# Seven-product block pairs in all output groups of a hybrid decoder layer

## The chip, the cores and the metric

The kernel runs on one core of a Trainium2 chip. The metric is the device time of one execution in microseconds (us). A fixed part of some 2 us lies around the span that the profiler records.

## The reference, cut to what matters

One decoder layer on 256 positions of width 4096, in float32:

```python
def hybrid_layer(x, norm_w, w_in, ..., w_out):
    h = rms_norm(x, norm_w)
    proj = jnp.einsum('bsd,de->bse', h, w_in)           # 4096 -> 13328 columns
    (rq, rk, rv, rg, mq, ..., lx, lg) = jnp.split(proj, ...)
    y_ret  = retention(rq, rk, rv, ret_gn_w) * silu(rg)
    y_moba = moba_attention(mq, mk, mv) * silu(mg)
    y_ssm  = mamba2_ssd(sz, sxbc, sdt, ...)
    y_lru  = rg_lru(lx, ...) * silu(lg)
    y = jnp.concatenate([y_ret, y_moba, y_ssm, y_lru], axis=-1)
    return x + jnp.einsum('bse,ed->bsd', y, w_out)      # 4096 -> 4096

# and behind the layer
out = rms_norm(x, final_norm_w)
```

The change lies in the last product, `y @ w_out`, and in what follows it.

## The kernel before, in words

Both large products keep float32 accuracy by splitting each operand into a high part of type fp32r and the rest (`xT` or `yhl` for the activations, `whi` and `wlo` for the weights). Each block product is then three matmuls: high by high, low by high, high by low. ScalarE (ACT) casts a raw weight tile to `whi` (L187), VectorE (DVE) subtracts to get `wlo` (L188), and TensorE (PE) runs the three matmuls of 128x128 weights by up to 512 columns.

The weights come as chunks of 256 rows by 512 columns (512 KB): two blocks of 128 rows side by side in a raw tile of 1024 columns. One list, `chunks`, holds them in the order of use. At each chunk the loop calls `split(n + SPL)`, which casts and subtracts the chunk two places ahead, and `load(n + RAW)`, which issues on SP's queue the DMA of the chunk four places ahead. There are `RAW` = 4 raw buffers and `SPL + 1` = 3 pairs `whi`, `wlo`. So a cast waits for the PE to leave the chunk before, and a load waits for the last reader of the raw buffer that it takes.

The output has eight groups of 512 columns (`o` = 0 to 7) with 16 chunks each, and two halves of 128 positions (`e` = 0, 1). In the order of time:

- Groups 0 and 1 run alone: per chunk 2 halves x 2 blocks x 3 = 12 matmuls. Between them `mix_y` forms from five chunks of `y` the sums that the pairs need (`ys`).
- Groups 2, 3 and 4, 5 run as pairs (`pair`), chunk by chunk. In 11 of the 16 chunks both groups take 12 matmuls each. In the five chunks of `FAST` = (2, 4, 7, 9, 12) the 2x2 block product (two blocks of rows by two groups, for two halves) is formed by seven block products in place of eight: 21 matmuls in place of 24 (Strassen's scheme in Winograd's form). For it DVE forms four sums of the raw weights in place (L177 to L180), and the two raw tiles are then cast and subtracted once more, whole, into `thi` and `tlo` (three buffers each). The products by themselves (`p1`, `p5`, `p6`, `p7`) gather in four PSUM banks of their own, the others in the four banks of the result. Behind the last such chunk `early` adds them to the residual tiles `xres`, two steps at each chunk (L843).
- Group 6 runs alone, then group 7 with a lag: its half `e` = 1 runs six chunks behind half 0, in pieces of 256 columns, from split tiles that are held (`hhi`, `hlo`), and six chunks of it are left when half 0 is done.

Each finished result goes through `row`: add to `xres` (DVE), square with a sum (ACT), multiply by the norm's weight into `rs` (DVE). At the end of a half, `store` gathers the sum, GpSimd (POOL) takes the power -1/2 (L803), DVE scales the half's 4096 columns in nine pieces (L806), and ACT and SP issue the DMAs of each piece to HBM.

The order of the instructions on each engine is set when the program is built: a scheduler places them from the program's order and its own costs, and each engine then runs its list in order.

Of the kernel before, what the change touches and what calls it, by code (L numbers as in the profile page):

```python
# [93 lines left out]
def tile_kernel(ctx: ExitStack, tc: tile.TileContext, t: dict):  # L94
# [64 lines left out]
    def split(n):  # L159
        if n >= len(chunks):  # L160
            return
        where, _, kt, nk, w = chunks[n]
# [3 lines left out]
        c = kt // KC
        pool, tag, bufs, size = wp, "w", SPL + 1, WW
        if where == "last" and c % (SPL + 1 + HOLD) > SPL:
            pool, tag, bufs, size = holds[0], "h", HOLD, KC * 512
# [582 lines left out]
    fsm = fp.tile([P, 64], F32, name="fsm")  # L752
# [26 lines left out]
    def mms(ps, e, c, p, c0=0, c1=512):  # L779
        hi, lo = p  # L780
        for k in range(KC):
            kt = c * KC + k
            x, a, b = yhl[kt], k * 512 + c0, k * 512 + c1
            xh, xl = x[:, e * P:(e + 1) * P], x[:, 256 + e * P:256 + (e + 1) * P]
            T.matmul(ps[:, c0:c1], xh, hi[:, a:b], start=kt == 0, stop=False)  # L785
            T.matmul(ps[:, c0:c1], xl, hi[:, a:b], start=False, stop=False)  # L786
            T.matmul(ps[:, c0:c1], xh, lo[:, a:b], start=False, stop=kt == KT - 1)  # L787
# [40 lines left out]
    def three(ps, x, p, at, first, last):  # L828

        hi, lo = p[0][:, at:at + 512], p[1][:, at:at + 512]  # L830
        T.matmul(ps, x[0], hi, start=first, stop=False)
        T.matmul(ps, x[1], hi, start=False, stop=False)
        T.matmul(ps, x[0], lo, start=False, stop=last)

    def pair(o, n, q, r):
# [147 lines left out]
```

## Time and profile before

| | |
|---|---|
| median of 3 runs | 1567.84 us (1567.80 to 1570.99) |
| the profiled execution | 1566.89 us |
| its span | 1565.1 us |
| PE busy | 1550.7 us, 99% |
| DVE busy | 910.9 us, 58% |
| ACT busy | 764.9 us, 49% |
| output product and what follows, within the span | from 1206.8 to 1565.1 us |

Matmuls are pipelined, and their ends are modelled: a matmul of 512 columns is shown with some 390 ns, while in an undisturbed stretch the next one starts 227 ns behind it. So the length of a stretch divided by its count of matmuls says more than the mean of one. The granted clock was at its upper level (1.00) throughout the products.

### The profile page before, as it was taken

What the parts mean: (1) busy time and instruction counts of PE and PEld (TensorE: products, weight loads), DVE (VectorE), ACT (ScalarE), POOL (GpSimd) and SP (SyncE); (2) the same over time, 40 slices, a digit from 0 to 9 for tenths busy, and PEclk for the clock granted to TensorE, in tenths of its full rate; (3) what the DMA queues carried; (4) which work ended last, traced back from release to release, by engine and by line L of the source; (5) the groups of instructions that cost most, each with busy time, mean ns of one, the idle gap of its engine ahead of it and who ended that gap; (6) DMA issues with size and microseconds to landing.
All of it is one profiled execution on the core that took longest, in us unless ns stands there. A gap on an engine that the chain in (4) does not pass through costs nothing.

```text
span 1565.1 us, 19219 instructions
## 1 busy us (share of the span) xinstructions
PE 1550.7 (99%) x7304; PEld 1292.6 (83%) x7304; DVE 910.9 (58%) x1132; ACT 764.9 (49%) x965; POOL 28.2 (2%) x56
## 2 busy tenths in 40 slices
PE   9999999999999999999999999999999999999997
PEld 8988888888888788888888888888888888777886
DVE  6564444475565644454557657444456747887754
ACT  6744444454454434444548845444446444554441
POOL 0000000000000100000000000000000000000000
PEclk9999999999999999999999999999999999999999
DMA  8965555555555655555555455555555666565763
GB/s 308 334 207 188 176 176 185 183 189 188 200 184 188 212 178 188 175 175 177 188 193 177 167 201 182 193 190 189 189 186 191 230 217 209 199 216 194 261 228 143
DMA packets 89133, 311.20 MB, mean 199 GB/s; under 512 B 10304, under 2 KB 11984, under 8 KB 89040
## 3 DMA queue, kind: packets, MB, share of 16 engines
q1 hardware_dynamic: 83808, 296.70, 54.9%
q0 software_dynamic: 3360, 10.51, 2.3%
q10 hardware_dynamic: 1872, 2.76, 0.5%
q8 instruction: 57, 0.93, 0.2%
q14 instruction: 36, 0.29, 0.1%
HBM read 305.71 MB, written 4.22 MB: 198 GB/s over the span
## 4 chain that ended last, share of the span: by engine, by line
PE 94%; DVE 2%; DMA 2%; ACT 1%; issue 1%; POOL 0%; ACTq 0%; POOLq 0%; DVEq 0%
PE pm L704 24%; PE pm L703 24%; PE pm L702 24%; PE pm L786 4%; PE pm L785 4%; PE pm L787 4%; PE pb L786 2%; PE pb L785 2%; PE pb L787 2%; PE pb L279 1%; DMA raw<-in_wo 1%; DVE wlo L188 1%; ACT whi L187 1%; PE pb L704 0%; PE pb L703 0%
## 5 line engine op out<-in xcount | busy, mean ns | idle before, releaser
L188 DVE TENSOR_TENSOR wlo<-raw,whi 128x1024 fp32r<-128x1024 f32 (+3 forms) x538 | 648.1, 1207 | 576.6 <-ACT whi L187 551.8
L187 ACT CAST whi<-raw 128x1024 fp32r<-128x1024 f32 (+3 forms) x538 | 556.1, 1035 | 678.8 <-PE pm L703 496.6
L702 PE MATMUL pm<-whi,xT 128*128 128x512 f32 (+1 forms) x1664 | 645.6, 388 | 1.4 <-ACT whi L187 1.4
L704 PE MATMUL pm<-wlo,xT 128*128 128x512 f32 (+1 forms) x1664 | 641.9, 386 | 0.8 <-DVE wlo L188 0.8
L703 PE MATMUL pm<-whi,xT 128*128 128x512 f32 (+1 forms) x1664 | 641.4, 386 | 0.0
L702 PEld LDWEIGHTS pm<-whi,xT 128*128 128x128 f32 x1664 | 312.7, 188 | 64.1 <-ACT whi L187 1.9
L704 PEld LDWEIGHTS pm<-wlo,xT 128*128 128x128 f32 x1664 | 312.2, 188 | 64.4 <-DVE wlo L188 1.6
L703 PEld LDWEIGHTS pm<-whi,xT 128*128 128x128 f32 x1664 | 312.6, 188 | 61.8
L786 PE MATMUL pm<-whi,xT 128*128 128x512 f32 (+1 forms) x252 | 95.7, 380 | 0.0
L787 PE MATMUL pm<-wlo,xT 128*128 128x512 f32 (+1 forms) x252 | 95.6, 379 | 0.0
L785 PE MATMUL pm<-whi,xT 128*128 128x512 f32 (+1 forms) x252 | 95.6, 379 | 0.0
L785 PE MATMUL pb<-whi,xT 128*128 128x512 f32 x152 | 59.2, 389 | 0.0
L786 PE MATMUL pb<-whi,xT 128*128 128x512 f32 x152 | 59.2, 389 | 0.0
L787 PE MATMUL pb<-wlo,xT 128*128 128x512 f32 x152 | 59.1, 389 | 0.0
L785 PEld LDWEIGHTS pm<-whi,xT 128*128 128x128 f32 x252 | 47.4, 188 | 9.0
L786 PEld LDWEIGHTS pm<-whi,xT 128*128 128x128 f32 x252 | 47.4, 188 | 9.0
L787 PEld LDWEIGHTS pm<-wlo,xT 128*128 128x128 f32 x252 | 47.4, 188 | 8.9
L785 PEld LDWEIGHTS pb<-whi,xT 128*128 128x128 f32 x152 | 28.5, 188 | 6.0
L787 PEld LDWEIGHTS pb<-wlo,xT 128*128 128x128 f32 x152 | 28.5, 188 | 5.9
L786 PEld LDWEIGHTS pb<-whi,xT 128*128 128x128 f32 x152 | 28.5, 188 | 5.9
L271 ACT ACTIVATE y<-pm,rstd 128x512 f32<-128x512 f32 x24 | 16.5, 687 | 14.7 <-PE pm L704 14.7
L188 DVE TENSOR_TENSOR tlo<-raw,thi 128x1024 fp32r<-128x1024 f32 x20 | 23.6, 1219 | 0.0
(272 smaller groups left out, 982.8 us busy)
## 6 DMA issues: line engine op xcount, KB each, us to landing
raw<-in_w SPq DMA_DIRECT2D x384, 512.0 KB, 3.5
raw<-in_wo SPq DMA_DIRECT2D x128, 512.0 KB, 4.4
raw<-in_w SPq DMA_DIRECT2D x31, 520.0 KB, 4.4
b<-in_x SPq DMA_DIRECT2D x8, 512.0 KB, 5.1
xres<-in_x POOLq DMA_DIRECT2D x16, 256.0 KB, 5.5
b<-in_xt SPq DMA_DIRECT2D x15, 257.0 KB, 4.5
fw<-in_fnw POOLq DMA_DIRECT2D x8, 256.0 KB, 5.7
out<-rs ACTq DMA_DIRECT2D x8, 256.0 KB, 2.9
```

The costliest lines, as they stand in the source:

```text
L187: A.copy(hi[:, a:b], raw[:, a:b])
L188: V.tensor_tensor(lo[:, a:b], raw[:, a:b], hi[:, a:b].bitcast(F32), ALU.subtract)
L271: A.activation(tk[k], ps[k], func, scale=rstd[:, k:k + 1])
L279: T.transpose(ps[:, e * S + k * P:e * S + (k + 1) * P], tk[k][:, (2 * u + e) * P:(2 * u + e + 1) * P], ident)
L702: T.matmul(ps[:, :w], xh, hi[:, o:o + w], start=first, stop=False)
L703: T.matmul(ps[:, :w], xl, hi[:, o:o + w], start=False, stop=False)
L704: T.matmul(ps[:, :w], xh, lo[:, o:o + w], start=False, stop=last)
L785: T.matmul(ps[:, c0:c1], xh, hi[:, a:b], start=kt == 0, stop=False)
L786: T.matmul(ps[:, c0:c1], xl, hi[:, a:b], start=False, stop=False)
L787: T.matmul(ps[:, c0:c1], xh, lo[:, a:b], start=False, stop=kt == KT - 1)
```

## The change

All eight output groups run as pairs (0 1, 2 3, 4 5, 6 7). Pair 0 has three chunks with seven products (7, 9, 12), the others five, 18 in all in place of 10. Chunks of both groups of a pair alternate in the list. `mix_y` runs at the chunks 1 to 5 of pair 0. The four banks for the result and the four for the separate products change places from pair to pair.

In a seven-product chunk the two raw sum tiles are cast and subtracted in halves of 512 columns, each as soon as its sum stands, into four buffers. There are five raw buffers in place of four, and room is made by a smaller area for the descriptors of POOL's DMAs (`dynamic_dma_scratch_size`).

Group 7 no longer runs with a lag. In the last pair the half `e` = 1 of the chunks 13 to 15 is left until half 0 is done (`held`): group 6 in whole rows of 512 columns, group 7 in two pieces of 256 in the banks `spare`. The rows of half 0 are finished and stored between.

```diff
-SPL, RAW, HOLD, WARM = 2, 4, 6, 28
+SPL, RAW, WARM = 2, 5, 28
-PAIRS, FAST = (2, 4), (2, 4, 7, 9, 12)
+FAST = {0: (7, 9, 12), 2: (2, 4, 7, 9, 12), 4: (2, 4, 7, 9, 12), 6: (2, 4, 7, 9, 12)}
+LATE = 13
...
+    for o in FAST:
+        for c in range(NCH):
+            for i in range(2):
+                where = "fast" + "ab"[i] if c in FAST[o] else "hold" if o == NO - 2 and LATE <= c + i / 2 < LATE + 1.5 else "out"
+                chunks.append((where, t["wo"][o + i, c], KC * c, KC, 512))
...
-            a = raws.pop("a")
-            V.tensor_tensor(a[:, 0:512], raw[:, 0:512], a[:, 0:512], ALU.subtract)
-            V.tensor_tensor(raw[:, 0:512], raw[:, 512:1024], raw[:, 0:512], ALU.subtract)
-            V.tensor_tensor(raw[:, 512:1024], raw[:, 512:1024], a[:, 0:512], ALU.subtract)
-            V.tensor_tensor(a[:, 512:1024], a[:, 512:1024], raw[:, 512:1024], ALU.subtract)
-            parts[n, "t"] = [high_low(r, ((0, 1024),), mixed[0], "t", 3, 1024) for r in (a, raw)]
...
+            ra, rb = raws.pop("a"), raw
+            (ha, la), (hb, lb) = (pair_of(mixed[0], "t", 4, 1024) for _ in range(2))
+            c1, c2 = slice(0, 512), slice(512, 1024)
+            V.tensor_tensor(ra[:, c1], rb[:, c1], ra[:, c1], ALU.subtract)
+            V.tensor_tensor(rb[:, c1], rb[:, c2], rb[:, c1], ALU.subtract)
+            high_low(ha, la, ra, 0, 512)
+            V.tensor_tensor(rb[:, c2], rb[:, c2], ra[:, c1], ALU.subtract)
+            high_low(hb, lb, rb, 0, 512)
+            V.tensor_tensor(ra[:, c2], ra[:, c2], rb[:, c2], ALU.subtract)
+            high_low(hb, lb, rb, 512, 1024)
+            high_low(ha, la, ra, 512, 1024)
+            parts[n, "t"] = (ha, la), (hb, lb)
...
-                if c not in FAST:
-                    for e in range(2):
-                        mms(q[2 * e + i], e, c, p)
-                    continue
...
+                else:
+                    mms(q[i], 0, c, p, c == 0, c == NCH - 1)
+                    if end and c >= LATE:
+                        held[c, i] = p
+                    else:
+                        mms(q[2 + i], 1, c, p, c == 0, c == (LATE - 2 if end and i else NCH - 1))
...
+        row(o, 0, q[0], x11, fw1, o)
+        row(o + 1, 0, q[1], x12, fw2, o + 1, 0, 256)
+        done = store(0)
+        row(o + 1, 0, q[1], x12, fw2, NO, 256, 512)
+        done()
+        for c in range(LATE, NCH):
+            mms(q[2], 1, c, held[c, 0], False, c == NCH - 1)
+        row(o, 1, q[2], x21, fw1, o)
+        for j, a in enumerate((0, 256)):
+            for c in range(LATE, NCH):
+                mms(spare[j], 1, c, held[c, 1], c == LATE, c == NCH - 1, a, a + 256)
+            row(o + 1, 1, spare[j], x22, fw2, NO if j else o + 1, a, a + 256)
+            if j == 0:
+                done = store(1)
+        done()
...
-    nc = bacc.Bacc("TRN2", target_bir_lowering=False, num_devices=1)
+    nc = bacc.Bacc("TRN2", target_bir_lowering=False, num_devices=1, dynamic_dma_scratch_size=4096)
```

DVE's list in the kernel before, from the splits ahead of a pair's first seven-product chunk on. The names are those of the sections above; L188 is the subtraction of a split, L177 to L180 are the four sums:

```order
L188 TENSOR_TENSOR wlo<-raw,whi 128x1024 x3
L177 TENSOR_TENSOR raw<-raw 128x512
L178 TENSOR_TENSOR raw<-raw 128x512
L188 TENSOR_TENSOR wlo<-raw,whi 128x512
L179 TENSOR_TENSOR raw<-raw 128x512
L180 TENSOR_TENSOR raw<-raw 128x512
L188 TENSOR_TENSOR wlo<-raw,whi 128x1024
L188 TENSOR_TENSOR tlo<-raw,thi 128x1024 x2
L188 TENSOR_TENSOR wlo<-raw,whi 128x1024 x2
```

The same place in the changed kernel, where L174 is the subtraction of a split and L186, L187, L189 and L191 are the sums:

```order
L174 TENSOR_TENSOR wlo<-raw,whi 128x1024 x3
L186 TENSOR_TENSOR raw<-raw 128x512
L187 TENSOR_TENSOR raw<-raw 128x512
L174 TENSOR_TENSOR wlo<-raw,whi 128x512
L174 TENSOR_TENSOR tlo<-raw,thi 128x512
L189 TENSOR_TENSOR raw<-raw 128x512
L174 TENSOR_TENSOR tlo<-raw,thi 128x512
L191 TENSOR_TENSOR raw<-raw 128x512
L174 TENSOR_TENSOR wlo<-raw,whi 128x1024
L174 TENSOR_TENSOR tlo<-raw,thi 128x512 x2
L174 TENSOR_TENSOR wlo<-raw,whi 128x1024 x2
```

The two whole subtractions into `tlo` became four halves, and two of them moved ahead of the last sums.

DVE's list in the changed kernel behind the last seven-product chunk of the last pair. `tlo` of 1024 columns are the held splits of the chunks 13 and 14, L843 are the additions of `early`:

```order
L174 TENSOR_TENSOR tlo<-raw,thi 128x1024
L843 TENSOR_TENSOR xres<-xres,ma 128x512
L174 TENSOR_TENSOR tlo<-raw,thi 128x1024
L843 TENSOR_TENSOR ma<-ma,pm 128x512
L174 TENSOR_TENSOR wlo<-raw,whi 128x1024
L843 TENSOR_TENSOR mb<-ma,pm 128x512
L174 TENSOR_TENSOR wlo<-raw,whi 128x1024
L843 TENSOR_TENSOR xres<-xres,ma 128x512
L174 TENSOR_TENSOR wlo<-raw,whi 128x1024
L843 TENSOR_TENSOR xres<-xres,pm 128x512
L843 TENSOR_TENSOR xres<-xres,mb 128x512 x2
L804 TENSOR_TENSOR xres<-xres,pb 128x512
```

In the kernel before, the splits at this place stood alone, with no additions between or behind them.

DVE's list in the kernel before from the first row piece of half 0 in group 7 on (L791 and L793 are the two DVE steps of `row`, L806 the scaling, `rs_9407` half 0 and `rs_9408` half 1):

```order
L791 TENSOR_TENSOR xres<-xres,pm 128x256
L793 TENSOR_TENSOR rs_9407<-xres,fw 128x256
L797 TENSOR_REDUCE fsm<-fsm 128x1
L791 TENSOR_TENSOR xres<-xres,pm 128x256
L798 TENSOR_SCALAR fsm<-fsm 128x1
L793 TENSOR_TENSOR rs_9407<-xres,fw 128x256
L802 TENSOR_TENSOR fsm<-fsm 128x1
L806 TENSOR_SCALAR rs_9407<-rs_9407,fsm 128x256 x2
L806 TENSOR_SCALAR rs_9407<-rs_9407,fsm 128x512 x7
L791 TENSOR_TENSOR xres<-xres,pm 128x256
L793 TENSOR_TENSOR rs_9408<-xres,fw 128x256
```

The same place in the changed kernel (L804, L806, L819 stand for L791, L793, L806; `rs_9409` is half 0, `rs_9410` half 1):

```order
L804 TENSOR_TENSOR xres<-xres,pb 128x256
L806 TENSOR_TENSOR rs_9409<-xres,fw 128x256
L810 TENSOR_REDUCE fsm<-fsm 128x1
L804 TENSOR_TENSOR xres<-xres,pb 128x256
L811 TENSOR_SCALAR fsm<-fsm 128x1
L804 TENSOR_TENSOR xres<-xres,pb 128x512
L806 TENSOR_TENSOR rs_9409<-xres,fw 128x256
L815 TENSOR_TENSOR fsm<-fsm 128x1
L806 TENSOR_TENSOR rs_9410<-xres,fw 128x512
L819 TENSOR_SCALAR rs_9409<-rs_9409,fsm 128x256 x2
L819 TENSOR_SCALAR rs_9409<-rs_9409,fsm 128x512 x7
L804 TENSOR_TENSOR xres<-xres,pm 128x256 x2
```

The row of half 1 in group 6 (L804 of 512 columns and its L806) now stands ahead of the scaling of half 0, and both row pieces of half 1 in group 7 behind it.

## Rows read from the trace of the kernel before

**Rows 1.** The page, its first part: busy time of each engine.

```profile
PE 1550.7 (99%) x7304; PEld 1292.6 (83%) x7304; DVE 910.9 (58%) x1132; ACT 764.9 (49%) x965; POOL 28.2 (2%) x56
```

**Rows 2.** Windows by stage; length, then PE, PEld, DVE, ACT, POOL busy (count).

```profile
1294.83:1380.03 85.20, 85.02 (x370) 68.13 (x369) 69.16 (x78) 43.58 (x51) 2.13 (x4) 1.00 0.60 206
1380.03:1466.29 86.26, 85.22 (x370) 68.09 (x369) 70.00 (x79) 43.70 (x51) 3.20 (x6) 1.00 0.63 213
1466.29:1509.81 43.52, 43.52 (x193) 36.04 (x192) 22.78 (x22) 19.23 (x22) 2.66 (x5) 1.00 0.66 230
1509.81:1545.05 35.24, 35.24 (x207) 31.18 (x206) 18.76 (x18) 14.79 (x17) 0.00 (x0) 1.00 0.49 166
1545.05:1555.05 10.00, 10.00 (x84) 9.85 (x83) 6.41 (x20) 1.53 (x6) 0.56 (x1) 1.00 0.56 212
1555.05:1565.10 10.05, 0.06 (x1) 0.00 (x0) 4.40 (x12) 0.51 (x2) 0.54 (x1) 0.66 0.55 209
```

**Rows 3.** Waits within the two pairs: total us, times, longest us.

```profile
PEld pb L831 <- ACT thi L187: 3.7, 10, 1.1
```

**Rows 4.** Timeline of PE in chunk 7 of the first pair; start, length.

```profile
1332.22 0.39 PE L831 MATMUL pm<-whi,xT 128*128 128x512 f32 x1
```

**Rows 5.** Timeline of PE in chunk 4 of the second pair.

```profile
1403.59 0.39 PE L833 MATMUL pm<-wlo,ys 128*128 128x512 f32 x1
1404.63 0.50 PE L831 MATMUL pb<-thi,ys 128*128 128x512 f32 x1 [0.65 <-ACT thi L187]
```

**Rows 6.** The chain of waits at the same place; start, length.

```profile
1394.77 5.22 DMA raw<-in_wo
...
1402.80 0.70 DVE raw L180
...
1403.53 1.05 ACT thi L187
```

**Rows 7.** Timeline of DVE around chunk 7 of the first pair.

```profile
1326.78 2.44 DVE L188 TENSOR_TENSOR wlo<-raw,whi 128x1024 fp32r<-128x1024 f32 x2 [2.40 <-ACT whi L187]
1329.25 0.69 DVE L177 TENSOR_TENSOR raw<-raw 128x512 f32<-128x512 f32 x1
1329.98 0.69 DVE L178 TENSOR_TENSOR raw<-raw 128x512 f32<-128x512 f32 x1
1330.59 0.68 DVE L188 TENSOR_TENSOR wlo<-raw,whi 128x512 fp32r<-128x512 f32 x1
1331.31 0.69 DVE L179 TENSOR_TENSOR raw<-raw 128x512 f32<-128x512 f32 x1
...
1334.42 2.35 DVE L188 TENSOR_TENSOR tlo<-raw,thi 128x1024 fp32r<-128x1024 f32 x2
1336.69 1.22 DVE L188 TENSOR_TENSOR wlo<-raw,whi 128x1024 fp32r<-128x1024 f32 x1
```

**Rows 8.** Timeline of DVE at the end of the first pair.

```profile
1380.46 1.28 DVE L791 TENSOR_TENSOR xres<-xres,pb 128x512 f32<-128x512 f32 x2
```

**Rows 9.** Timeline of DVE at the end of the kernel.

```profile
1545.07 0.42 DVE L791 TENSOR_TENSOR xres<-xres,pm 128x256 f32<-128x256 f32 x1 [4.84 <-PE pm L787]
...
1547.19 0.16 DVE L802 TENSOR_TENSOR fsm<-fsm 128x1 f32<-128x1 f32 x1 [0.18 <-ACT pm L792]
1548.04 3.39 DVE L806 TENSOR_SCALAR rs<-rs,fsm 128x256 f32<-128x256 f32 x9 [0.68 <-POOL fsm L803]
1551.34 0.41 DVE L791 TENSOR_TENSOR xres<-xres,pm 128x256 f32<-128x256 f32 x1
...
1556.14 0.16 DVE L802 TENSOR_TENSOR fsm<-fsm 128x1 f32<-128x1 f32 x1
1556.96 3.39 DVE L806 TENSOR_SCALAR rs<-rs,fsm 128x256 f32<-128x256 f32 x9 [0.66 <-POOL fsm L803]
```

**Rows 10.** Timeline of POOL, its longest run of DMAs.

```profile
520.46 2.12 POOL L475 DMA_DIRECT2D qk<-csd  x4
```

**Rows 11.** The page, its last part: these DMAs; size, time from issue to landing.

```profile
qk<-csd POOLq DMA_DIRECT2D x8, 192.0 KB, 5.8
```

More of the change, by code (lines that the diff above doesn't have):

```diff
@@ L165, in split, with high_low @@
         raw = raws.pop(n)
[L166 to L169, printed above, removed]
+        if where == "hold":
+            hi, lo = pair_of(mixed[0], "t", 4, 1024)
+        else:
+            hi, lo = pair_of(wp, "w", SPL + 1, WW)
+        parts[n] = hi, lo
+        def high_low(h, l, raw, a, b):
+            A.copy(h[:, a:b], raw[:, a:b])
+            V.tensor_tensor(l[:, a:b], raw[:, a:b], h[:, a:b].bitcast(F32), ALU.subtract)
         cuts = FIRST if n == 0 else CUTS if n == 1 else ((512, 1024),) if where == "fastb" else ((0, nk * w),)
-        parts[n] = high_low(raw, cuts, pool, tag, bufs, size)
+        for a, b in cuts:
+            high_low(hi, lo, raw, a, b)
         if where == "fasta":
@@ L196, in pcol @@
         return par[:, PCOL[name][0] + i:PCOL[name][0] + i + n]
-    xT, holds, mixed = [], [], []
+    xT, mixed = [], []
     def split_x(raw):
@@ L751, in tile_kernel @@
     fp = ctx.enter_context(tc.tile_pool(name="fp", bufs=1))
[L752 removed]
+    fsm = fp.tile([P, 176], F32, name="fsm")
     fss = fsm[:, 0:2 * (NO + 1)].rearrange("p (a b) -> p a b", a=2)
@@ L777, in mix_y, with three, tile_y, mms @@
         ysum[c] = hl
-    def mms(ps, e, c, p, c0=0, c1=512):
-        hi, lo = p
-        for k in range(KC):
[L782 to L787, printed above, removed]
+    def three(ps, x, p, at, first, last):
+        w = ps.shape[-1]
+        hi, lo = p[0][:, at:at + w], p[1][:, at:at + w]
+        T.matmul(ps, x[0], hi, start=first, stop=False)
+        T.matmul(ps, x[1], hi, start=False, stop=False)
+        T.matmul(ps, x[0], lo, start=False, stop=last)
+    def tile_y(kt, e):
+        return yhl[kt][:, e * P:(e + 1) * P], yhl[kt][:, 256 + e * P:256 + (e + 1) * P]
+    def mms(ps, e, c, p, first=False, last=False, a=0, b=512):
+        for k in range(KC):
+            three(ps[:, a:b], tile_y(KC * c + k, e), p, k * 512 + a, first and k == 0, last and k == KC - 1)
     def row(o, k, ps, xres, fw, at, a=0, b=512):
@@ L826, in extra, with pair @@
         return fw, xres
[L828 to L835, printed above, removed]
+    side = collections.deque()
+    def pair(o, n, q, r, spare):
         more = [extra(o), extra(o + 1)]
-        (x11, x21), (x12, x22) = more[0][1], more[1][1]
+        (fw1, (x11, x21)), (fw2, (x12, x22)) = more
         p1, p5, p6, p7 = r
-        side = collections.deque()
+        fast, end = FAST[o], o == NO - 2
+        held = {}
         def add(out, a, b):
@@ L857, in early @@
             add(x22, x22, p5)
+            if end:
+                add(x22, x22, q[3])
         for c in range(NCH):
+            if o == 0 and 1 <= c <= len(MIX):
+                mix_y(MIX[c - 1])
             for i in range(2):
@@ new lines, in pair @@
+                if c == fast[-1] and i == 1:
+                    early()
+        while side:
+            side.popleft()()
+        if not end:
+            for i in range(2):
+                for e in range(2):
+                    row(o + i, e, q[2 * e + i], more[i][1][e], more[i][0], o + i)
+            return n
+        row(o, 0, q[0], x11, fw1, o)
[3 more added lines that the diff above has]
+        done()
@@ L936 @@
+    for j, o in enumerate(FAST):
+        pools = (pm, "pm"), (pb, "pb")
+        q, r = ([p.tile([P, 512], F32, name=name) for _ in range(4)] for p, name in pools[::-1 if j % 2 else 1])
+        n = pair(o, n, [q[0], q[2], q[1], q[3]], r, r[:2])
 def kernel(**inputs):
```

98 lines of the change are left out of this document (17 added, 81 removed).

## The prediction, made before the changed kernel ran

> **What bounds the kernel now.** I read the busy times first: PE is busy 99% of the span, DVE 58%, ACT 49% [rows 1]. So a gain has to come out of PE's list or out of the stretch behind it, and DVE has room on the mean. Next the windows by stage, for what a matmul takes and where PE loses time [rows 2]. Group 6 is undisturbed: 192 matmuls of 512 columns in 43.52 us, 0.2267 each. The 84 matmuls of 256 columns behind 1545.05 take 10.00 us, 0.119 each, more than half of the long ones. A pair has 11 x 24 + 5 x 21 = 369 matmuls, by 0.2267 83.64 us. The first pair takes 85.20 and the second 86.26, so 1.56 and 2.62 us are lost, 4.18 over ten seven-product chunks. Then the waits, for the cause: PE's weight loads wait ten times in each pair for the cast `thi` (those of the second: 3.7 us, longest 1.1) [rows 3]. The timeline shows the worst: one matmul starts at 1403.59, the next at 1404.63, which is 0.81 more than 0.23 [rows 5]. The chain of waits tells why: the raw chunk landed 5.22 us after a raw buffer had come free, four sums followed on DVE, and only behind the last did `thi` start, at 1403.53 [rows 6]. Last I read the end: PE leaves half 0 at 1545.05, ends at 1555.05, and the span ends 10.05 later [rows 2].
>
> **PE's list.** Eight more seven-product chunks, three matmuls less in each: 24 x 0.2267 = 5.44 us. The pieces of 256 columns shrink from 192 to 36. Group 7 took 35.24 + 10.00 = 45.24 us, of which 96 matmuls are whole ones, 21.76; so 192 pieces took 23.48. As 96 whole ones they would take 21.76. Of these 18 turn into 36 pieces at 0.119, 4.28 in place of 4.08. Gain 23.48 - 21.76 - 0.20 = 1.52. Together 6.96 us less on PE, the engine that sets the time up to 1545.
>
> **What the seven-product chunks lose.** In the old order `thi` begins behind the last of four sums. Now its first half needs only the first sum, and DVE's next steps are one piece each. I set DVE's steps against PE in chunk 7 of the first pair. PE enters it at 1332.22 [rows 4]; DVE is done with its first split and starts the sums at 1329.25, 2.97 earlier [rows 7]. Start to start, a sum or a split of 512 columns takes 0.61 to 0.73 (1329.25, 1329.98, 1330.59, 1331.31), one of 1024 takes 1.14 (1334.42 to 1336.69 for two). In the new order DVE then stands, from PE's entry, at 1.86 (four sums, one chunk split and two pieces of `tlo` done), 3.00 (the next chunk's split), 3.61 and 4.22 (the last two pieces). PE wants the first piece of `tlo` at 2.49 and the second at 3.17, well behind them; the last two at 3.85 and 4.53, with results at 3.70 and 4.30. So all four are in time, the last by some 0.2 us. What is left is the small loss that every chunk shows; I take 0.15. In the chunks 4 and 9, which follow a seven-product chunk by two, the last cast stands behind the next chunk's, and the last piece comes at about 4.6, so I take 0.3. The fifth raw buffer serves these: their first chunk loads early, and only the second waits for a buffer, free at 4.3 of the chunk before. With 5.22 us its raw tile would stand 0.6 before PE comes, too late for sums that start 2.97 ahead. But the 5.22 were two loads on each other's heels; I expect the first alone at some 2.6. Sum 11 x 0.15 + 7 x 0.3 = 3.75 for 18 chunks, against 4.18: a gain of 0.43. The bounds: nothing lost at all, 0; and the second pair's mean, 2.62 / 5 = 0.52 in each, 9.4.
>
> [...]
>
> **Mixes, rows and loads.** `mix_y` runs as before beside normal chunks, which leave DVE idle half the time (22.78 of 43.52 busy in group 6 [rows 2]). Three pairs now end in front of another pair, as the first did; rows of 1.2 us per two operations [rows 8] then lie between the splits, and PE's list showed no gap there. I cost both at nothing; without that cover each boundary would lose one row operation, 0.6. POOL's smaller descriptor area is tried by its longest run, four and four DMAs at 0.53 us each [rows 10]; they land 5.8 us later [rows 11], so at least eight were under way. If they still fit, nothing; if one had to land before the next, the last would be 8 x 5.8 - 10 = 36 us late. I take nothing, since later DMAs come in threes.
>
> **The end.** Here DVE becomes the bound. I count from PE's entry into chunk 12 of the last pair. PE leaves it at 4.9. The chunks 13 to 15 then hold only half 0: six steps of 6 matmuls, 1.36 us each, to 13.07. DVE is done with the sums' pieces at 4.22 as above, then has five splits of 1.14 and four additions of `early` of 0.61 between them: 12.5. PE waits for the last split and leaves half 0 at 13.5. Behind it DVE has seven more operations of 512 columns (0.63) before the first row piece of group 7: 16.9. The two pieces took 2.12 to L802 (1545.07 to 1547.19 [rows 9]); with one row step of half 1 now between them, at 0.65 and partly in the waits for ACT, 19.5. From L802 to the scaling 0.85, the scaling 3.30 (1548.04 to 1551.34): 23.6. Only then come the last two row pieces of half 1, though PE has had them ready since 13.5 + 4.08 + 4.28 = 21.9: 2.1 more, 25.7. From L802 to the scaling 0.82 (1556.14 to 1556.96), from there to the end 8.14: 34.7. That is 21.6 behind PE's undisturbed 13.07. Before, it was 1565.10 - 1545.05 = 20.05. So the end costs 1.55 more, with PE's wait in it.
>
> **Sum.** PE has 10.00 us of matmuls behind half 0 before, 8.36 after; so half 0 is left 6.96 + 0.43 - 1.64 = 5.75 earlier, and the span ends 5.75 - 1.55 = 4.2 earlier. From the profiled execution's 1566.89 that is 1562.7; its median of three runs stands 0.95 higher, which gives 1563.6. I forecast 1563.4 us. The case's own range takes 0 to 0.4 us per seven-product chunk and half a microsecond at the end: 1560.5 to 1566.
>
> **Rivals.**
> - *DVE falls behind in every seven-product chunk, and the kernel gets slower.* Two chunks of the pattern cost DVE, by full durations, 1.22 + 9 x 0.69 + 2 x 1.22 = 9.9 us, against PE's 45 matmuls, 10.2. It decides when the last piece of `tlo` is over 0.2 us later than worked out; the chunk split in front of it and the casts on ACT add to it. At the second pair's 0.52 the loss is 9.4 in place of 3.75: 1569.1, slower by 0.1%. At the 0.81 of its worst chunk everywhere 14.6: 1574. For it: 0.2 us of room is little. Against it: no chunk in either pair lost more through `tlo` than the last ones did through `thi`, and that wait is taken apart.
> - *The end stays on PE.* If DVE's additions find gaps (they are placed one by one, and some could go ahead of a waiting split), the end is PE's 13.07 + 8.36 = 21.43, and 10.05 behind it as now: 31.5, 3.2 earlier than above. Result 1560.2. Against it: DVE's list has no idle step between 0 and 17, as I count it.
> - *The additions and rows at the end cost more.* If the last splits also wait for their loads (three chunks of 512 KB at 1.36 us per step, where one load took up to 5.22), each late load holds a split: 1 to 2 us more, 1565.4, no change that can be measured.
> - *POOL's DMAs queue up.* Up to 36 us late at 520 us; some 11 us of slack lie in four chunk steps, so up to 1588.
>
> **How the numbers follow.** A difference of 0.2%, 3.1 us, is about what a measurement of this kernel tells from none. Forecast 0.55, of which four fifths lie over 3.1 us faster; the end on PE 0.14, all faster; DVE behind in every chunk 0.14, half of it within 0.2%, half slower; a dearer end 0.14, within; POOL 0.03, slower. So faster 0.44 + 0.14 = 0.58, same 0.11 + 0.07 + 0.14 = 0.32, slower 0.10. The range, 1560.2 to 1569.2, reaches from the end on PE to the second pair's rate in all chunks, and leaves out the worst chunk's rate and POOL.
>
> **What would show it.** Each step is right if: windows of the middle pairs have 369 matmuls in some 84.7 us, with no wait for `thi` over 0.1 us; DVE, not PE, runs without idle time from chunk 12 of the last pair to the scaling of half 0; the scaling of half 1 begins within 1 us of the last row operations, some 5 us behind PE's last matmul (now 1.9); half 0 is left near 1539.5. It is wrong if weight loads wait for `tlo` by tenths in most chunks, if PE shows gaps at the pairs' boundaries, or if the start of the kernel, where only the fifth load differs, moves by more than a few tenths.

## The result, and the profile after

The changed kernel took 1559.05 us (median of 6 runs, 1557.91 to 1560.3) against 1567.6 for the kernel before (6 runs): ratio 0.9945, 95% interval [0.9932, 0.9958]. So it is faster, by 8.5 us; the forecast was 4.2 to 4.4, and the time lies 1.15 below the range of 1560.2 to 1569.2. The profiled execution took 1558.47 with a span of 1556.7, 8.4 less than before.

The busy line and the windows of the changed kernel answer to [rows 1, 2]: one window for each pair, then from PE's last step of half 0 to its last matmul, then the rest. The last three figures of a window are the granted clock, the DMA engines' busy share and GB/s.

```profile
PE 1541.6 (99%) x7202; PEld 1286.7 (83%) x7202; DVE 954.6 (61%) x1233; ACT 779.3 (50%) x1019; POOL 28.7 (2%) x56
```

```profile
1207.23:1293.25 86.02, 86.02 (x384) 71.09 (x383) 71.99 (x109) 44.62 (x60) 3.74 (x7) 1.00 0.62 214
1293.25:1376.89 83.64, 83.64 (x370) 69.26 (x369) 70.07 (x89) 44.29 (x61) 3.20 (x6) 1.00 0.63 220
1376.89:1460.53 83.64, 83.64 (x370) 69.26 (x369) 70.08 (x89) 44.30 (x61) 3.21 (x6) 1.00 0.65 221
1460.53:1536.03 75.50, 75.50 (x334) 62.47 (x333) 64.27 (x82) 41.04 (x55) 2.67 (x5) 1.00 0.59 202
1536.03:1544.43 8.40, 8.40 (x55) 7.64 (x53) 7.79 (x21) 2.36 (x8) 0.94 (x1) 1.00 0.06 23
1544.43:1556.70 12.27, 0.15 (x2) 0.00 (x0) 6.69 (x21) 0.91 (x4) 0.54 (x1) 0.70 0.86 328
```

The second line is the main reading: 369 matmuls of 0.22667 are 83.64 us, and the pair takes 83.64. The seven-product chunks lose nothing; before, the two pairs lost 1.56 and 2.62. (The first pair's 86.02 are 1.02 more than its 375 matmuls take: eight matmuls of 128 columns, the last of the stage before, run within its chunk 0. The kernel before has 1.04 there.) The last line is 12.27 where 10.05 stood.

The cause stands in DVE's timeline around chunk 7 of the first middle pair (start, length, line), which answers to [rows 7]; PE enters the chunk at 1329.97 (second fence).

```profile
1326.85 0.69 DVE L186 TENSOR_TENSOR raw<-raw 128x512 f32<-128x512 f32 x1
1327.57 0.69 DVE L187 TENSOR_TENSOR raw<-raw 128x512 f32<-128x512 f32 x1
1328.18 0.69 DVE L174 TENSOR_TENSOR wlo<-raw,whi 128x512 fp32r<-128x512 f32 x1
1328.78 0.69 DVE L174 TENSOR_TENSOR tlo<-raw,thi 128x512 fp32r<-128x512 f32 x1
1329.38 0.68 DVE L189 TENSOR_TENSOR raw<-raw 128x512 f32<-128x512 f32 x1
1329.99 0.68 DVE L174 TENSOR_TENSOR tlo<-raw,thi 128x512 fp32r<-128x512 f32 x1
1330.59 0.68 DVE L191 TENSOR_TENSOR raw<-raw 128x512 f32<-128x512 f32 x1
1331.19 1.22 DVE L174 TENSOR_TENSOR wlo<-raw,whi 128x1024 fp32r<-128x1024 f32 x1
1332.33 1.28 DVE L174 TENSOR_TENSOR tlo<-raw,thi 128x512 fp32r<-128x512 f32 x2
```

```profile
1329.97 0.39 PE L790 MATMUL pm<-whi,xT 128*128 128x512 f32 x1
...
1331.79 0.39 PE L792 MATMUL pb<-wlo,ys 128*128 128x512 f32 x1
1332.01 0.39 PE L790 MATMUL pm<-thi,ys 128*128 128x512 f32 x1
1332.24 0.39 PE L791 MATMUL pm<-thi,ys 128*128 128x512 f32 x1
```

The first two sums stand 0.72 apart, the steps that alternate between tiles 0.60 to 0.61. The last piece of `tlo` is done 1332.33 + 1.28 - 1329.97 = 3.64 after PE's entry; I had worked out 4.30, and PE wants it at 4.53. PE goes on to `thi` in 0.22 to 0.23, where [rows 5] had a gap of 1.04. Within 1293 to 1536 no wait of PE or of a weight load on `thi` or `tlo` is left. Of the waits for raw loads, the first line is the kernel before in its first pair alone, the second all that remains in the changed kernel within 1293 to 1536 (total us, times, longest):

```profile
ACT whi L187 <- DMA raw<-in_wo: 18.8, 12, 2.6
ACT whi L173 <- DMA raw<-in_wo: 2.3, 3, 1.3
```

At the end, DVE's timeline answers to [rows 9].

```profile
1533.68 1.23 DVE L174 TENSOR_TENSOR wlo<-raw,whi 128x1024 fp32r<-128x1024 f32 x1
1534.82 0.68 DVE L843 TENSOR_TENSOR xres<-xres,pm 128x512 f32<-128x512 f32 x1
...
1539.02 0.41 DVE L804 TENSOR_TENSOR xres<-xres,pb 128x256 f32<-128x256 f32 x1
...
1541.41 0.16 DVE L815 TENSOR_TENSOR fsm<-fsm 128x1 f32<-128x1 f32 x1
...
1542.63 3.39 DVE L819 TENSOR_SCALAR rs<-rs,fsm 128x256 f32<-128x256 f32 x9 [0.46 <-POOL fsm L816]
1545.93 0.75 DVE L804 TENSOR_TENSOR xres<-xres,pm 128x256 f32<-128x256 f32 x2
...
1547.71 0.16 DVE L815 TENSOR_TENSOR fsm<-fsm 128x1 f32<-128x1 f32 x1
1548.53 3.39 DVE L819 TENSOR_SCALAR rs<-rs,fsm 128x256 f32<-128x256 f32 x9 [0.66 <-POOL fsm L816]
```

From 1519.97 to 1541.4 DVE has no idle step. The scaling of half 1 begins 4.1 behind PE's last matmul, where 1.9 stood before: the end is DVE's.

### The profile page after: what moved, and what is told of

Its sections match the earlier page's. It is cut to its first block, busy times and chain, and to the rows that moved or that the text cites. A ratio compares the mean times of both kernels' runs of the same rounds, so it can differ in the third digit from the quotient of the medians.

```text
span 1556.7 us, 19182 instructions
## 1 busy us (share of the span) xinstructions
PE 1541.6 (99%) x7202; PEld 1286.7 (83%) x7202; DVE 954.6 (61%) x1233; ACT 779.3 (50%) x1019; POOL 28.7 (2%) x56
## 4 chain that ended last, share of the span: by engine, by line
PE 97%; DVE 1%; issue 1%; DMA 0%; ACT 0%; POOL 0%; ACTq 0%; POOLq 0%; DVEq 0%
PE pm L712 24%; PE pm L710 24%; PE pm L711 24%; PE pm L792 4%; PE pm L790 4%; PE pm L791 4%; PE pb L791 3%; PE pb L792 3%; PE pb L790 3%; PE pb L287 1%; PE pb L711 0%; PE pb L712 0%; PE pb L710 0%; DMA b<-in_xt 0%; DVE xres L843 0%
## 5 line engine op out<-in xcount | busy, mean ns | idle before, releaser
L174 DVE TENSOR_TENSOR wlo<-raw,whi 128x1024 fp32r<-128x1024 f32 (+3 forms) x545 | 650.7, 1198 | 540.3 <-ACT whi L173 518.1
L710 PE MATMUL pm<-whi,xT 128*128 128x512 f32 (+1 forms) x1664 | 645.7, 388 | 1.1 <-ACT whi L173 1.1
L712 PE MATMUL pm<-wlo,xT 128*128 128x512 f32 (+1 forms) x1664 | 642.4, 386 | 0.9 <-DVE wlo L174 0.9
L711 PE MATMUL pm<-whi,xT 128*128 128x512 f32 (+1 forms) x1664 | 641.7, 386 | 0.0
L712 PEld LDWEIGHTS pm<-wlo,xT 128*128 128x128 f32 x1664 | 312.5, 188 | 64.5 <-DVE wlo L174 1.7
L710 PEld LDWEIGHTS pm<-whi,xT 128*128 128x128 f32 x1664 | 312.9, 188 | 63.6 <-ACT whi L173 1.6
L711 PEld LDWEIGHTS pm<-whi,xT 128*128 128x128 f32 x1664 | 312.8, 188 | 62.0
L791 PE MATMUL pm<-whi,xT 128*128 128x512 f32 (+1 forms) x218 | 84.1, 386 | 0.0
L790 PE MATMUL pm<-whi,xT 128*128 128x512 f32 (+1 forms) x218 | 84.0, 385 | 0.0
L792 PE MATMUL pm<-wlo,xT 128*128 128x512 f32 (+1 forms) x218 | 84.0, 385 | 0.0
L791 PE MATMUL pb<-whi,xT 128*128 128x512 f32 x178 | 69.2, 389 | 0.0
L792 PE MATMUL pb<-wlo,xT 128*128 128x512 f32 x178 | 69.2, 389 | 0.0
L790 PE MATMUL pb<-whi,xT 128*128 128x512 f32 x178 | 69.2, 389 | 0.0
L173 ACT CAST thi<-raw 128x512 fp32r<-128x512 f32 (+1 forms) x75 | 45.8, 636 | 33.1 <-DVE raw L186 19.9
L174 DVE TENSOR_TENSOR tlo<-raw,thi 128x512 fp32r<-128x512 f32 (+1 forms) x75 | 52.0, 708 | 0.2
L790 PEld LDWEIGHTS pm<-whi,xT 128*128 128x128 f32 x218 | 41.0, 188 | 8.2
L791 PEld LDWEIGHTS pm<-whi,xT 128*128 128x128 f32 x218 | 41.0, 188 | 8.2
L792 PEld LDWEIGHTS pm<-wlo,xT 128*128 128x128 f32 x218 | 41.0, 188 | 8.1
L791 PEld LDWEIGHTS pb<-whi,xT 128*128 128x128 f32 x178 | 33.4, 188 | 7.0
L792 PEld LDWEIGHTS pb<-wlo,xT 128*128 128x128 f32 x178 | 33.4, 188 | 7.0
L790 PEld LDWEIGHTS pb<-whi,xT 128*128 128x128 f32 x178 | 33.4, 188 | 7.0
```

The costliest lines, as they stand in the source:

```text
L173: A.copy(h[:, a:b], raw[:, a:b])
L174: V.tensor_tensor(l[:, a:b], raw[:, a:b], h[:, a:b].bitcast(F32), ALU.subtract)
L710: T.matmul(ps[:, :w], xh, hi[:, o:o + w], start=first, stop=False)
L711: T.matmul(ps[:, :w], xl, hi[:, o:o + w], start=False, stop=False)
L712: T.matmul(ps[:, :w], xh, lo[:, o:o + w], start=False, stop=last)
```

## Experiments: where the loss went

"Loss" is the time of a chunk from its first matmul to the next chunk's, less 0.22667 for each of its matmuls. The middle pairs are the groups 2, 3 and 4, 5, the last pair is 6, 7. The kernels start from the changed one, but for the two that are said to start from the kernel before.

**Fifth buffer undone.**

```diff
-SPL, RAW, WARM = 2, 5, 28
+SPL, RAW, WARM = 2, 4, 28
```

> The changed kernel with four raw buffers in place of five; pieces of 512 columns stay. In the changed kernel the four pairs lose 0.0 us to waits in their seven-product chunks (369 matmuls in 83.64 us). Theory A, the pieces alone did it: the loss stays under 0.5 us in all 18 chunks together, 1559 us. Theory B, the fifth buffer alone did it: 0.4 us per chunk come back, as in the kernel before, 7.5 in all, 1566.5 us. Theory C, each does its share: the chunks 4 and 9 (seven of the 18), whose first load now waits for the chunk two before, lose some 0.5 each, 3.5 in all, 1562.5 us.

1568.74 us, ratio to the kernel before 0.9998 [0.9987, 1.0009]. The middle pairs lose 1.95 and 2.46 (chunk 4: 1.19 and 1.17, chunk 9: 0.50 and 0.61), the last pair 3.75, more than half of it (2.19) in chunks 13 to 15; chunk 7 loses 0.04. The windows of the two middle pairs, against 83.64:

```profile
1294.18:1379.78 85.60, 84.89 (x371) 69.04 (x369) 69.42 (x89) 44.88 (x61) 3.21 (x6) 1.00 0.65 216
1379.78:1465.88 86.10, 85.10 (x370) 68.96 (x369) 69.42 (x89) 44.87 (x61) 3.20 (x6) 1.00 0.63 214
```

So the chunks 4 and 9 lose as theory C expected, and more, but chunk 2 of the second middle pair (0.48) and the last pair's end lose too, which theory C left out: the whole gain is gone.

**Pieces undone.**

```diff
-            high_low(ha, la, ra, 0, 512)
...
-            high_low(hb, lb, rb, 0, 512)
...
-            high_low(hb, lb, rb, 512, 1024)
-            high_low(ha, la, ra, 512, 1024)
+            high_low(ha, la, ra, 0, 1024)
+            high_low(hb, lb, rb, 0, 1024)
```

> The changed kernel with five raw buffers, but the two sum tiles are cast and subtracted whole (1024 columns) behind the last of the four sums, as before. Theory A (pieces alone): 0.2 to 0.4 us are lost in each of the 18 chunks, since the cast again begins behind the last sum, 4 to 7 us in all, 1563 to 1566 us. Theory B (buffer alone): under 0.5 us in all, 1559 us. Theory C: 0.2 in each chunk as in the undisturbed ones before, 4 in all, 1563 us.

1563.74 us, 0.9968 [0.9957, 0.9978]. Nearly every seven-product chunk loses 0.19 to 0.22 (the last one of the last pair 0.41), the chunks 4 and 9 no more than the others. The waits of this kernel in its middle pairs, and PE in chunk 7 of the first:

```profile
PEld pm L788 <- ACT thi L173: 2.2, 10, 0.3
PEld pb L788 <- ACT thi L173: 2.2, 10, 0.3
PEld pm L790 <- DVE tlo L174: 1.0, 5, 0.2
PEld pb L790 <- DVE tlo L174: 1.0, 5, 0.2
```

```profile
1333.62 0.39 PE L790 MATMUL pb<-wlo,ys 128*128 128x512 f32 x1
1333.85 0.49 PE L788 MATMUL pm<-thi,ys 128*128 128x512 f32 x1
1334.17 0.39 PE L789 MATMUL pm<-thi,ys 128*128 128x512 f32 x1
```

In each chunk two weight loads wait for `thi` and one for `tlo`, some 0.2 each. The first matmul on `thi` takes 0.32 in place of 0.227, and the next ten or so 0.22 to 0.26. This is the "small loss that every chunk shows" of the prediction: not a cost of the form, but a cast that begins only behind the last sum.

**Both undone** (the two edits above together).

> The changed kernel with four raw buffers and whole sum tiles, so that only the pairs and the end are new. All three theories: the loss per chunk is that of the kernel before, 0.42 on the mean, 7.5 us over 18 chunks, 1566.5 us. If it is far less, the order in which PE takes the products (program order now, mixed with the next chunk before) is a cause of its own.

1572.64 us, 1.0022 [1.0009, 1.0034]. The middle pairs lose 3.94 and 2.35, the last 5.36. Pairs everywhere with old splits and four buffers are slower than the kernel before. From here the pieces alone give 3.9 and the buffer alone 8.9. Both give 13.6 by the medians, but the changed kernel's median is of another series; by the ratios to the kernel before it is 12.1, and by the losses in the profiles 12.6.

**The same two edits on the kernel before.** Both runs also have the smaller area for POOL's descriptors.

```diff
-SPL, RAW, HOLD, WARM = 2, 4, 6, 28
+SPL, RAW, HOLD, WARM = 2, 5, 6, 28
```

> The kernel before with a fifth raw buffer (and the smaller descriptor area) and nothing else. Theory (two separate losses: a cast behind four whole sums costs about 0.2 in every seven-product chunk; the late load costs more in the chunks 4 and 9 only, and the fifth buffer takes that away): the two pairs lose 1.1 us each in place of 1.56 and 2.62, so 2.0 us less, near 1566 (ratio 0.9987). Rival (the late load and the late cast are one loss, the buffer alone changes nothing): 4.2 lost, ratio 1.000. Second rival (the whole loss was the loads): no loss left, 4.2 us less, ratio 0.9973.

```diff
-            parts[n, "t"] = [high_low(r, ((0, 1024),), mixed[0], "t", 3, 1024) for r in (a, raw)]
+            (ha, la), (hb, lb) = ([mixed[0].tile([P, 1024], F32R, name="t" + x, bufs=4) for x in ("hi", "lo")] for _ in range(2))
...
+            piece_split(ha, la, ra, 0, 512)
...
+            piece_split(ha, la, ra, 512, 1024)
```

> The kernel before with the sums in pieces of 512 columns and nothing else (four raw buffers). Theory: the undisturbed seven-product chunks lose nothing (0.22 before), but the chunks 4 and 9 keep their late load, 0.5 to 1.2 each as in the changed kernel with four buffers; the pairs lose 1.9 to 2.5 each, 4.4 in all against 4.2: ratio 1.000. Rival (the pieces and the buffer each give half of the gain, whatever the other does): 2.0 us less, ratio 0.9987.

Windows of the two pairs, first with the fifth buffer alone, then with the pieces alone:

```profile
1295.87:1380.75 84.88, 84.88 (x370) 67.88 (x369) 69.23 (x78) 42.87 (x51) 2.13 (x4) 1.00 0.61 208
1380.75:1465.56 84.81, 84.81 (x370) 67.87 (x369) 70.00 (x79) 43.00 (x51) 3.20 (x6) 1.00 0.63 217
```

```profile
1295.90:1380.82 84.92, 84.26 (x371) 69.09 (x369) 68.57 (x88) 44.98 (x61) 2.14 (x4) 1.00 0.61 207
1380.82:1465.88 85.06, 84.34 (x371) 69.05 (x369) 69.44 (x89) 45.10 (x61) 3.19 (x6) 1.00 0.63 217
```

Less 83.64, the buffer leaves 1.24 and 1.17, that is 0.21 to 0.26 in each chunk: near the 1.1 expected. The pieces leave 1.28 and 1.42, nearly all of it in the chunks 4 and 9 (0.56, 0.66; 0.80, 0.57): the place expected, but 2.7 and not 4.4, so the theory mis-sized it. Of the 4.2 before, 2.4 are thus late casts in ten chunks, which stay when the loads are in time, and 1.8 go with the late loads. The pieces alone take only 1.5 away, since a late load makes the pieces late too. One such place, chunk 4 of the first pair with the pieces alone:

```profile
1321.29 0.39 PE L843 MATMUL pb<-thi,xT 128*128 128x512 f32 x1
1321.96 0.50 PE L844 MATMUL pb<-tlo,xT 128*128 128x512 f32 x1 [0.29 <-DVE tlo L181]
1322.30 0.39 PE L796 MATMUL pb<-whi,xT 128*128 128x512 f32 x1
```

The times, 1566.31 us, 0.9993 [0.9983, 1.0002], and 1566.6 us, 0.9997 [0.9987, 1.0007], cannot tell 2 us from none, the more so as both output products start 1.05 later than in the kernel before.

**Four buffers, once more, the tiles moved.** In the run with four buffers all tiles behind the raw buffers had moved too. Here they stand at multiples of 512 bytes again.

```diff
-SPL, RAW, WARM = 2, 5, 28
+SPL, RAW, WARM = 2, 4, 28
...
-    fsm = fp.tile([P, 176], F32, name="fsm")
+    fsm = fp.tile([P, 192], F32, name="fsm")
```

> The changed kernel with four raw buffers once more, but with the small tile in front of the output product's tiles 64 bytes longer, so that the sums' tiles and the mixes stand at multiples of 512 bytes again (in the earlier run with four buffers they stood 448 bytes off). Theory (the loss there was late loads in the chunks 4 and 9 and in the last chunks): the same losses, 1.9 and 2.4 us in the middle pairs, 3.7 in the last, 1568.7. Rival (part of it was the place of the tiles): the small 0.04 of undisturbed seven-product chunks goes, the chunks 4 lose 0.5 to 0.8 as in the kernel before with pieces alone (0.56 and 0.80), so 1.3 to 1.4 in each middle pair and under 2 in the last: 1564 to 1565.

1569.0 us, 1.0 [0.9991, 1.001]: the rival's 1564 to 1565 did not come. The undisturbed chunks' 0.04 is gone, but the middle pairs lose 2.68 and 2.17, the last pair 2.26 in place of 3.75. All losses come to 7.7 against 8.8 in the first run with four buffers, so by these two profiles the place of the tiles accounts for about 1 us at most. The time doesn't show it, since the output product starts 1.65 later here. The chain of waits at chunk 4 of its first middle pair shows how:

```profile
1299.92 7.73 DMA raw<-in_wo
...
1307.75 1.06 ACT whi L173
...
1310.09 3.45 DMA raw<-in_wo
...
1313.92 1.06 ACT whi L173
...
1315.01 1.24 DVE wlo L174
```

The two loads land 7.73 and 3.45 after their buffers came free. DVE starts the sums at 1316.27 and PE enters the chunk at 1317.19, so they are 0.92 ahead. In the changed kernel they start at 1310.15, 4.18 ahead of PE's entry at 1314.33. Casts waited for raw loads 21 times, 44.5 us in the two pairs.

## Experiments: the end, and how far it goes

**An even spacing.** Seven-product chunks at 6, 8, 10 and 2, 4, 6, 8, 10, their number unchanged; the last one is earlier by two chunks, and so is the early addition.

```diff
-FAST = {0: (7, 9, 12), 2: (2, 4, 7, 9, 12), 4: (2, 4, 7, 9, 12), 6: (2, 4, 7, 9, 12)}
+FAST = {0: (6, 8, 10), 2: (2, 4, 6, 8, 10), 4: (2, 4, 6, 8, 10), 6: (2, 4, 6, 8, 10)}
...
-            if end:
-                add(x22, x22, q[3])
...
-                        mms(q[2 + i], 1, c, p, c == 0, c == (LATE - 2 if end and i else NCH - 1))
+                        mms(q[2 + i], 1, c, p, c == 0, c == (LATE - 1 if end and i else NCH - 1))
...
+                if end and c == LATE - 1 and i == 1:
+                    add(x22, x22, q[3])
```

> The changed kernel with its seven-product chunks at 6, 8, 10 (pair 0) and 2, 4, 6, 8, 10 (the others) in place of 7, 9, 12 and 2, 4, 7, 9, 12; the additions behind the last of them are then done before the short steps of the last three chunks. Same count of matmuls. Theory, DVE bounds the end by its additions: the stretch behind PE's last matmul falls from 12.27 to some 10.1 us, 1557 us. Rival, something else bounds the end (the two scalings or the output DMAs): it stays at 12 us or more, 1559. Rival on the chunks: with every second chunk a seven-product one DVE has 9.9 us of work in PE's 10.2 without a rest, falls behind, and 0.3 us or more are lost in the later chunks, 3 us in all, 1560 to 1562.

1556.6 us, 0.992 [0.9897, 0.9942]. No seven-product chunk loses anything, and the stretch behind PE's last matmul is 10.15 in place of 12.27; its scaling of half 1 starts 2.0 behind PE:

```profile
1544.70:1554.85 10.15, 0.13 (x2) 0.00 (x0) 4.54 (x14) 0.51 (x2) 0.54 (x1) 0.66 0.68 259
```

```profile
1546.69 3.39 DVE L819 TENSOR_SCALAR rs<-rs,fsm 128x256 f32<-128x256 f32 x9 [0.66 <-POOL fsm L816]
```

So the end of the changed kernel was bound by DVE's additions, and with them out of the way it is PE's again.

**Two seven-product chunks in a row** (3 in place of 4, in three pairs).

```diff
-FAST = {0: (6, 8, 10), 2: (2, 4, 6, 8, 10), 4: (2, 4, 6, 8, 10), 6: (2, 4, 6, 8, 10)}
+FAST = {0: (6, 8, 10), 2: (2, 3, 6, 8, 10), 4: (2, 3, 6, 8, 10), 6: (2, 3, 6, 8, 10)}
```

> The even spacing of two, but chunk 3 in place of chunk 4 is a seven-product chunk, in three pairs: two of them follow each other directly, as many matmuls as before. Theory (DVE needs about 7 us of starts for a seven-product chunk with its splits, PE 4.76; what DVE has in advance, some 4 us at PE's entry, does not cover two in a row): the last pieces of chunk 3 come at about 5.4 from PE's entry, wanted at 3.85 and 4.53, so 1 to 1.6 us lost in each of three pairs, 1559.6 to 1561.5 against 1556.6. Rival (DVE's advance covers two in a row): 1556.6, no loss. Second rival (late loads follow, as the raw buffers come free later): 2.5 and more per pair, over 1564.

1559.55 us, 0.9957 [0.994, 0.9973]. Chunk 3 alone loses, 0.47, 0.95 and 0.55: DVE does fall behind there (its sums start 0.55 ahead of PE, where those of chunk 2 start 3.1 ahead), but by about half of what I worked out.

**Six in a pair.** First with narrower buffers of the split weights, to make room for a sixth mix.

```diff
-RW, WW = 1040, 1152
+RW, WW = 1040, 1040
...
-    fsm = fp.tile([P, 176], F32, name="fsm")
+    fsm = fp.tile([P, 64], F32, name="fsm")
...
+FAST = {0: (6, 8, 10, 12), 2: (2, 4, 6, 8, 10, 12), 4: (2, 4, 6, 8, 10, 12), 6: (2, 4, 6, 8, 10)}
```

> Seven-product chunks at an even spacing of two, with one more in each of the first three pairs (chunk 12): 21 in place of 18. Theory (at a spacing of two DVE keeps up, about 9.4 us of starts against PE's 10.2 in two chunks): nine matmuls of 0.2267 less, 2.0 us, and loss still under 0.1 per pair: 1554.6 against 1556.6 of the even spacing with 18 (ratio to the kernel before 0.991). Rival (DVE's room is used up by the sixth in a row): 0.3 to 0.8 lost in the last chunks of each pair, 1556 to 1557, no gain.

1579.54 us, 1.0078 [1.0063, 1.0093]: neither. The output product already starts at 1226.1 and not near 1207, and normal chunks lose as much as the others: matmuls are slower throughout. A kernel with the width alone settles that:

```diff
-RW, WW = 1040, 1152
+RW, WW = 1040, 1040
...
-    fsm = fp.tile([P, 176], F32, name="fsm")
+    fsm = fp.tile([P, 208], F32, name="fsm")
```

> The even spacing with 18 seven-product chunks, where only the split weights' tiles are 1040 columns wide in place of 1152: they stand at 0, 64, 128, 192, 256 and 320 bytes past a multiple of 512, everything else that the matmuls read stands at multiples of 512. Theory (a matmul is slower when the tile it streams and the tile it loads as weights stand at different places modulo 512 bytes; this made the run with six seven-product chunks 1.2% slower): matmuls of 512 columns take 0.231 in place of 0.2267 over the whole program, some 20 us more: 1575 to 1578 against 1556.6. Rival (it was the sixth chunk, or the chip's state in that run): 1556.6.

1580.66 us, 1.008 [1.0065, 1.0095]: the sixth chunk is innocent. A middle pair of it, and the same with 1152 columns (83.63 us for the same 369 matmuls at the same granted clock, 1.00):

```profile
1312.91:1398.06 85.15, 85.15 (x370) 69.32 (x369) 71.43 (x89) 44.94 (x61) 3.19 (x6) 1.00 0.64 216
```

```profile
1293.52:1377.15 83.63, 83.63 (x370) 69.28 (x369) 71.21 (x89) 44.87 (x61) 3.21 (x6) 1.00 0.66 220
```

Then six at the old width; the sixth mix and, later, the last 1024 columns of half 0's rows share a tile.

```diff
+TAIL = {0: 12}
...
+    rs = [fp.tile([P, 3072 if k in TAIL else D], F32, name=f"rs{k}") for k in range(2)]
...
+                tails[k] = mixed[0].tile([P, 1024], F32R, name=f"ys{c}")
```

> 21 seven-product chunks at a spacing of two (chunk 12 added in the first three pairs), with the widths as in the changed kernel; the sixth mix lies where the last 1024 columns of half 0's result come to lie later. Theory (DVE keeps up at a spacing of two; the slow run with six came from the tiles' places alone): nine matmuls less, 2.0 us: 1554.6 against 1556.6, no loss over 0.1 in a pair. Rival (DVE's room is used up by the sixth): 0.3 to 0.8 lost at each of three pairs' ends, 1555.5 to 1557.

1555.49 us, 0.9919 [0.9902, 0.9935]. Both middle pairs take 82.96 us, which is 366 matmuls without any loss: DVE keeps up with six at a spacing of two, at 75.9 us busy in 82.96.

```profile
1294.19:1377.15 82.96, 82.96 (x367) 68.74 (x366) 75.93 (x97) 46.34 (x65) 3.20 (x6) 1.00 0.65 222
```

The output product up to PE's last matmul is 335.19 us against 337.21 with five. The whole time is 1.1 below the even spacing's, on another chip and with a start 1.34 later; the runs can't tell that much from nothing.

**Seven in a pair** (12 and 14 added in the first three).

```diff
-FAST = {0: (6, 8, 10, 12), 2: (2, 4, 6, 8, 10, 12), 4: (2, 4, 6, 8, 10, 12), 6: (2, 4, 6, 8, 10)}
+FAST = {0: (6, 8, 10, 12, 14), 2: (2, 4, 6, 8, 10, 12, 14), 4: (2, 4, 6, 8, 10, 12, 14), 6: (2, 4, 6, 8, 10)}
...
-TAIL = {0: 12}
+TAIL = {0: 12, 1: 14}
```

> 24 seven-product chunks: 12 and 14 added in the first three pairs, 18 matmuls less than with the even spacing of 18 chunks. Theory (behind chunk 14 only one chunk is left for the eight operations of the early addition and the first row operations; these and four chunk splits are some 9 us of DVE in the 10.2 that PE has up to the next pair's first chunk, whose banks they must free): PE waits 0.5 to 2 us at each of three boundaries, 1554 to 1558. Rival (there is room, as at the other boundaries): 1552.5.

1555.81 us, 0.9921 [0.9906, 0.9936]: nine matmuls fewer than with six, and no gain: the output product up to PE's last matmul takes 335.86. The pairs behind a boundary lose 0.16, 1.41 and 0.68 (0.52 of the last in its chunk 12, where PE waits for `wlo`), and the first pair 0.45 in its chunk 8. The second of them starts at 1376.11, and DVE's timeline still has the early addition (L850) and the rows (L808, L810) there:

```profile
1377.79 0.68 DVE L850 TENSOR_TENSOR xres<-xres,pm 128x512 f32<-128x512 f32 x1
1378.38 1.28 DVE L808 TENSOR_TENSOR xres<-xres,pb 128x512 f32<-128x512 f32 x2
1379.58 1.29 DVE L810 TENSOR_TENSOR rs<-xres,fw 128x512 f32<-128x512 f32 x2
```

The loss shows later, in chunk 3 (1.36), where PE waits for `thi`: the backlog reaches the next sums, which start 1.0 ahead of PE's entry into chunk 2 in place of 3.1, and not the banks as the theory had it. Five evenly spaced, six and seven in a pair (1556.6, 1555.49 and 1555.81) are the fastest versions found, and the runs don't tell them apart.

## Why the prediction was wrong

Measured on the prediction's own sum, in the profiled executions: half 0 was left 1545.05 - 1536.03 = 9.02 earlier (5.75 forecast), and from there the end took 20.67 against 20.05, 0.62 more (1.55 forecast). 9.02 - 0.62 = 8.40, the gain in the span; 4.2 was forecast. The 4.2 between them are 3.75 of loss that did not come and 0.93 less at the end, less 0.48 of later start.

- **PE's list: right.** 24 matmuls and the 256-column pieces, 6.96. The matmuls behind half 0 took 8.40 (8.36 worked out).
- **What the seven-product chunks lose: the step that failed.** "What is left is the small loss that every chunk shows; I take 0.15", and 0.3 in the chunks 4 and 9: 3.75 in 18 chunks, where 0.00 was measured. This is 3.75 of the 4.2 by which the forecast missed. The direction was right and my own positions said that all pieces come in time; then I added a loss that I had not explained. The 0.22 of undisturbed chunks stood in [rows 3] as ten waits, and the kernel with whole pieces brings it back: it is the wait for the late `thi`, and goes with it. The positions were also too late, 4.30 for 3.64, mostly because I took 0.69 for a step where alternating ones start every 0.60; the sums also start 3.12 ahead of PE and not 2.97. Two more pieces in a chunk cost DVE by these very steps 4 x 0.61 - 2 x 1.14 = 0.16 to 4 x 0.73 - 2 x 1.14 = 0.64, and 0.12 by the measured 0.60. In the chunks 4 and 9 I expected sums 2.97 ahead of PE; with the fifth buffer they start 3.9 to 4.2 ahead. The fifth buffer, for which the sum had no term, is the larger part: 8.9 us from the kernel with both undone, where the pieces give 3.9.
- **Mixes, rows, loads, POOL's DMAs at nothing: right.** No gap at the pairs' boundaries, and no stretch of the size that queued DMAs would have cost: the last of the eight DMAs in a row landed 6.21 behind its issue (6.17 before).
- **The end: right in kind, dearer by 0.9 than it was.** From PE's entry into chunk 12 (1460.53 + 276 x 0.22667 = 1523.09) I had the last split done at 12.5, the first 256-column row at 16.9, the scaling of half 0 over at 23.6 and the end at 34.7. Measured: 11.8, 15.9, 22.8 and 33.6. PE did not wait for the last split: it left half 0 at 12.94 (13.07 undisturbed, 13.5 forecast). The even spacing shows that the bound was DVE.
- **The start: missed by 0.48.** The output product starts at 1207.23 against 1206.75. Over the kernels at full width it lay between 1206.75 and 1209.22, with no relation to the number of buffers that I can see. Every kernel with the smaller descriptor area starts the output product later than the kernel before, by 0.17 to 2.47, and the area was not tried alone; but 0.34 of the 0.48 stand long before the longest run of POOL's DMAs, at one that POOL issues at 251.00, before at 250.66. The cause stays open.
- **The rivals.** DVE falling behind needs what the changed kernel avoids: two seven-product chunks in a row, or an early addition with one chunk left. The end on PE came about only with the even spacing. The dearer end by late loads is what four buffers would have given: 2.19 in the chunks 13 to 15 in the first run with four, 0.99 in the second. The range's lower end was set by the wrong case, the end on PE with the 3.75 still in it, 1560.2; the bound of 0 for that loss alone, which the text names, gives 1563.4 - 3.75 = 1559.65. The other range, 1560.5 to 1566, does not follow from its own terms either: 0 to 0.4 us per chunk and half a microsecond at the end give 1559.15 to 1567.35.

## What to carry to other kernels

A small loss that repeats in every undisturbed step, like the 0.22 here, is to be taken for a wait until the trace shows otherwise: look for its releaser before it is carried over as a constant, and ask whether the change moves that releaser. When a chain of loads, sums and casts feeds TensorE, cutting the chain into pieces and buying one more buffer for its head are two different cures. On the kernel before each alone left about 1.2 to 1.4 us per pair; in the changed kernel the buffer alone left 1.1 in a middle pair, the pieces alone 2.0 to 2.7, and both left none. What DVE finished late at the end was moved by placing the last seven-product chunk, and with it the early addition, two chunks earlier, at no cost in work: the stretch behind PE's last matmul fell from 12.27 to 10.15 us.
